# A 31-tap convolution as float32 column-group products on TensorE, and new x made tile by tile behind a normed output

## The chip, the core and the metric

The kernel runs on one core of one Trainium2 chip. The metric is the device time of one launch in microseconds (us), the median of several runs. The core has TensorE for matrix products, VectorE, ScalarE and GpSimd for elementwise work, and SyncE, whose queue here issues the DMA transfers. The profile calls them PE (PEld for its weight loads), DVE, ACT, POOL and SP.

## The reference, cut to what matters

Two transformer blocks run one after the other on x of 512 tokens by 1024 channels. Block 1 has three parts, each followed by a norm of its output and an addition to x; block 2 has six (half-weighted swiglu layers, a pooling mixer and latent attention), added without such a norm.

```python
def first_block(x, mem, ...):
    h = rmsnorm(x, norm_mix_pre)
    y = parallel_mixer(h, ...)
    x = x + rmsnorm(y, norm_mix_post)
    h = rmsnorm(x, norm_mem_pre)
    y = memory_cross_attention(h, rmsnorm(mem, mem_norm_g), ...)
    x = x + rmsnorm(y, norm_mem_post)
    h = rmsnorm(x, norm_ffn_pre)
    y = conv_gated_ffn(h, ...)
    x = x + rmsnorm(y, norm_ffn_post)

def parallel_mixer(h, w_in, conv_dw, conv_dw_b, ...):
    z = h @ w_in
    a = a_val * sigmoid(a_gate)               # 512 channels of z
    a = dwconv_centred(a, conv_dw, conv_dw_b) # depthwise, 31 taps, centred
    a = silu(layernorm(a, ...))
    q, k = rope(rmsnorm(q, ...)), rope(rmsnorm(k, ...))
    att = gqa(q, k, v)                        # 8 heads, 2 kv heads
    return concat([a, att]) @ w_out
```

## The kernel before

Activations lie with channels on the partitions: x is eight tiles of 128 channels by 512 tokens. A product is made from exact parts: a float32 operand is split into a high part `hi` that fp32r keeps, and the rest `lo`, and `mm3` sums three matmuls (hi·hi, hi·lo, lo·hi). Weights come from DRAM in units of 128 x 1024 (`fetch`, on SP's queue, into three buffers `raw`); `cook` makes `hi` on ACT and `lo` on DVE or, for a share of `wshare` fourths of the units, on POOL (`W_IN`, `W_KV`: all of them for the in-projection and for the memory's keys and values). `linear` runs over output tiles, and each of them over the input tiles.

**The mixer** first makes 14 output tiles of the in-projection (`ORDER`): four pairs of gate and value, whose product is the convolution's input `at`, one tile of k, one of v, four of q. Then come eight heads of attention, one head ahead: `scores` (products, maximum on DVE, exponential on ACT), `attend` (transposes and products on PE). Between the heads stand two units of the memory's key and value projection (`mem_kv`, after `mem_prep`), and at the end the product with `w_out`. The convolution has four channel tiles. Of the 31 taps of a tile six are PE products with diagonal matrices (`conv_pe`, tile `dg` from POOL), one is an ACT operation and 24 are DVE operations of the form acc = at * w + acc (`conv_taps`). It is a generator, a tap a step; `step` takes six taps behind every output tile of the in-projection, 30 behind the last, eight behind each head, and `issue_after` pins them behind a named instruction. `conv_norm` follows, at the heads `CN_AT`.

**Behind each of block 1's three parts** stands a settling. `post_collect` evacuates the part's output as y (times the norm's gain) with its squares; `settle`, called from `pre` of the next part, sums the squares on PE, makes the reciprocal root on DVE in 4-column operations, and broadcasts it with four PE products into PSUM (`bc`). ACT copies this to SBUF (`rs`); DVE makes y·rs of tiles 0 and 1 and POOL those of tiles 2 to 7; DVE adds each y to its x tile. `split` then makes `xh` (ACT) and `xl` (DVE), ACT makes the squares and POOL adds them up (`gather`). While PE waits it runs 25 bf16 products that nobody reads (`warm`). The order of work on each engine comes from the scheduler, within these dependences.

The lines of the profile's rows are the 24 taps' line (`acc` from `at`, `cwh`), the diagonals' line (`dg`), the addition in `settle` (`x` from `x`, `y`), the low part in `split_into` (`xl`), and the low part of weights in `cook` (`wlo`).

Of the kernel before, what the change touches and what calls it, by code (L numbers as in the profile page):

```python
# [17 lines left out]
P = 128  # L18
# [8 lines left out]
# order of the taps' offsets: the even ones from the middle, then the odd ones  # L27
TAPS = sorted(range(-(KTAPS // 2), KTAPS // 2 + 1), key=lambda d: (d % 2, abs(d), d))
# [5 lines left out]
_VECS = [  # L34
    ("g_mix", 8), ("conv_w", 4 * KTAPS), ("conv_b", 4), ("cln_g", 4), ("cln_b", 4),
# [25 lines left out]
class Kern:  # L61
# [3 lines left out]
    def __init__(self, ctx, tc, a, out):  # L65
# [10 lines left out]
                      for n, b in (("xs", 16), ("cv", 9), ("pr", 2), ("m", 16), ("q", 17), ("t", 7),  # L76
                                   ("tb", 4))}
# [25 lines left out]
    # -- small access helpers --  # L103
# [10 lines left out]

    def ps(self, tag="ps", name="ps"):
        return self.pps[tag].tile([P, S], F32, name=name, tag=tag)
# [40 lines left out]
    def load_tile(self, w, nt, nk):  # L157
        """Stationary tiles of output tile nt: list over k of (hi, lo) [P, P]."""
# [6 lines left out]
    def mm3(self, ps, w, x, start, stop):  # L165
        """ps += w.T @ x with w, x each given as exact (hi, lo) parts."""
# [14 lines left out]
    # -- split an fp32 tile (SBUF or PSUM), optionally scaled per partition --  # L181
# [31 lines left out]
    def columns(self, sm, dim, eps=0.0, w=1):  # L213
        """sm / dim + eps in columns [P, block, w], in PSUM."""
# [8 lines left out]
    def newton(self, v, n):  # L223
        """rsqrt of v [P, n] on the vector engine."""
# [14 lines left out]
    def rstd(self, sqs, dim, nb=4):  # L239
        """rsqrt(mean + eps) in columns from squares [P, nb * P], summed over the list."""  # L240
        sm = self.sums([(self.c("ones"), sq) for sq in sqs], nb)
# [26 lines left out]
    def bcast_ps(self, R, nb=4, w=1):  # L268
        """Columns to rows of all partitions (row r of w in its share of them), exact float32."""
# [14 lines left out]
    def expand(self, R, w, tag="t"):  # L284
        """Columns -> [32 * block + r, tokens], zero outside the block, as exact parts."""
# [13 lines left out]
    def spread(self, X, r, tag="mi"):  # L299
        """Row r of every block, on all partitions."""  # L300
# [6 lines left out]
    # -- residual stream --  # L307
# [5 lines left out]
    def gather(self, sqs, sq, last, w=S):  # L313
        """Sum of squares so far: at most two tiles, the last one kept apart."""
# [5 lines left out]

    def pre(self, gname, dve_squares=(), tag2="xs"):
# [27 lines left out]
    def settle(self):  # L349
        """Generator: adds the pending normed output to x, a tile a step."""  # L350
# [22 lines left out]
    SETTLE = 2  # L373
# [32 lines left out]
    def rope(self, src, g, gs, cos, sin):  # L406
        """Rotary embedding along the partitions (pairs 16 apart), gains g, gs folded in."""
# [11 lines left out]
    def stack(self, src, r, tag, on_pool=False):  # L419
        """Exact parts of the 64 rows src[64 r:], one in each half of a tile."""  # L420
# [27 lines left out]
    def mem_prep(self):  # L448
        """Gain times memory as exact parts."""
# [14 lines left out]
    def mem_kv(self):  # L464
        """Generator: key and value projections of the memory, a weight unit a step."""
# [927 lines left out]
```

## Time and profile before

| | |
|---|---|
| time, median of 3 runs | 2588.05 us (2588.05 to 2589.86) |
| span of the profiled execution | 2588.3 us |
| PE busy | 2496.1 us, 96% of the span |
| DVE busy | 1385.5 us, 54% |
| ACT busy | 919.1 us, 36% |
| POOL busy | 521.8 us, 20% |
| mixer (start to the last product with `w_out`) | 0 to 321 us |
| first settling | 321 to 354 us |
| memory part | to 460 us |
| second settling | 460 to 497 us |
| conv-gated feed-forward | to 841 us |
| third settling | 841 to 878 us |
| block 2 | to 2588 us |

Matmuls are pipelined: the record of a 512-column matmul is 0.39 us long, while the next one starts about 0.23 us later, so the share of busy time says only where PE stood still, and the granted clock (PEclk, 1.00 is 2.4 GHz, 0.50 is 1.2 GHz) where it ran slowly. A float32 matmul leaves two records, an fp32r one a single record. Idle time is listed with the instruction that ended it.

### The profile page before, as it was taken

How to read it: one execution, taken by the hardware profiler on the slowest of the kernel's cores; microseconds unless marked ns; L12 is line 12 of the kernel's file. 1: busy time of each engine (PE TensorE's matmuls, PEld its weight loads, DVE VectorE, ACT ScalarE, POOL GpSimd, SP SyncE). 2: the span in 40 equal slices, each digit the busy share in tenths (PEclk: the TensorE clock that was granted, in tenths of full speed). 3: DMA queues.
4: the chain of work that ended last, by engine and by line, in shares of the span. 5: the costliest groups of instructions: out<-in, count | busy, mean ns of one | idle time of the engine just before them, and what ended most of it. 6: DMA issues, size and time to landing. Idle time of an engine off the chain costs nothing.

```text
span 2588.3 us, 29365 instructions
## 1 busy us (share of the span) xinstructions
PE 2496.1 (96%) x11668; PEld 2037.2 (79%) x11668; DVE 1385.5 (54%) x1877; ACT 919.1 (36%) x1332; POOL 521.8 (20%) x417
## 2 busy tenths in 40 slices
PE   7879989899999899999999999999999999999999
PEld 6667768688888688888888888888887778888887
DVE  7997563686632645533655543555433576555522
ACT  3336534354422333322422322323222455422221
POOL 4575232311100311101211100111000144111100
PEclk9889999999999999999999999999999999999999
DMA  4211211133333222234232333223332210333232
GB/s 163 66 67 49 90 57 58 64 98 98 96 95 97 69 94 96 95 98 132 74 98 98 97 98 96 97 95 95 98 98 88 78 62 19 104 98 97 92 107 79
DMA packets 68201, 229.80 MB, mean 89 GB/s; under 512 B 7456, under 2 KB 9632, under 8 KB 68064
## 3 DMA queue, kind: packets, MB, share of 16 engines
q1 hardware_dynamic: 66688, 225.35, 27.1%
q0 software_dynamic: 1232, 2.36, 0.3%
q8 instruction: 91, 1.49, 0.2%
q14 instruction: 46, 0.38, 0.0%
q10 hardware_dynamic: 144, 0.23, 0.0%
HBM read 225.80 MB, written 2.10 MB: 88 GB/s over the span
## 4 chain that ended last, share of the span: by engine, by line
PE 86%; DVE 4%; ACT 1%; issue 0%; ACTq 0%
PE ps L169 26%; PE ps L168 26%; PE ps L170 26%; DVE x L369 1%; DVE xl L190 1%; PE wo L168 1%; PE wo L169 1%; PE wo L170 1%; PE pt L124 1%; PE po L169 0%; PE bc L274 0%; PE po L168 0%; PE po L170 0%; PE sc L168 0%; DVE wlo L140 0%
## 5 line engine op out<-in xcount | busy, mean ns | idle before, releaser
L138 ACT CAST whi<-raw 128x1024 fp32r<-128x1024 f32 (+2 forms) x432 | 440.5, 1021 | 1217.7 <-PE ps L169 767.5
L140 DVE TENSOR_TENSOR wlo<-raw,whi 128x1024 fp32r<-128x1024 f32 (+2 forms) x400 | 559.3, 1400 | 492.6 <-ACT whi L138 487.5
L169 PE MATMUL ps<-xl,whi 128*128 128x512 f32 x2008 | 789.8, 394 | 18.6 <-DVE xl L190 18.5
L168 PE MATMUL ps<-xh,whi 128*128 128x512 f32 x2008 | 784.9, 393 | 15.0 <-ACT xh L189 14.7
L170 PE MATMUL ps<-xh,wlo 128*128 128x512 f32 x2008 | 786.6, 392 | 0.0
L169 PEld LDWEIGHTS ps<-xl,whi 128*128 128x128 f32 x2008 | 380.5, 189 | 104.6 <-DVE xl L190 25.0
L168 PEld LDWEIGHTS ps<-xh,whi 128*128 128x128 f32 x2008 | 379.7, 189 | 97.3 <-ACT xh L189 16.2
L170 PEld LDWEIGHTS ps<-xh,wlo 128*128 128x128 f32 x2008 | 380.7, 190 | 79.8 <-issue 0.9
L168 PE MATMUL ps<-ah,whi 128*128 128x512 f32 x880 | 342.3, 389 | 0.0
L169 PE MATMUL ps<-al,whi 128*128 128x512 f32 x880 | 342.3, 389 | 0.0
L170 PE MATMUL ps<-ah,wlo 128*128 128x512 f32 x880 | 342.3, 389 | 0.0
L877 DVE TENSOR_TENSOR g<-ps,bct 128x512 f32<-128x512 f32 x176 | 120.6, 691 | 389.9 <-PE ps L170 382.8
L882 POOL TENSOR_TENSOR g<-g 128x512 f32<-128x512 f32 x88 | 119.0, 1353 | 856.5 <-ACT whi L138 457.6
L317 POOL TENSOR_TENSOR sq<-sq 128x512 f32<-128x512 f32 x72 | 112.7, 1566 | 535.8 <-ACT sq L310 533.9
L170 PEld LDWEIGHTS ps<-ah,wlo 128*128 128x128 f32 x880 | 165.2, 188 | 34.4
L169 PEld LDWEIGHTS ps<-al,whi 128*128 128x128 f32 x880 | 165.2, 188 | 34.2
L168 PEld LDWEIGHTS ps<-ah,whi 128*128 128x128 f32 x880 | 165.2, 188 | 34.2
L556 DVE SCALAR_TENSOR_TENSOR acc<-at,cwh,acc 128x502 f32<-128x502 f32 (+12 forms) x96 | 114.1, 1201 | 1.0 <-ACT acc L548 0.5
L140 POOL TENSOR_TENSOR wlo<-raw,whi 128x1024 fp32r<-128x1024 f32 x32 | 81.3, 2542 | 71.4 <-ACT whi L138 71.2
L185 ACT CAST ah<-g 128x512 fp32r<-128x512 f32 x88 | 54.7, 622 | 112.8 <-POOL g L882 112.8
L387 DVE SCALAR_TENSOR_TENSOR x<-ps,x 128x512 f32<-128x512 f32 x40 | 27.5, 691 | 84.5 <-PE ps L170 84.4
L858 POOL TENSOR_TENSOR c<-c 128x512 f32<-128x512 f32 x22 | 29.7, 1348 | 208.3 <-DVE c L845 178.5
(298 smaller groups left out, 2594.8 us busy)
## 6 DMA issues: line engine op xcount, KB each, us to landing
raw<-in_wgu SPq DMA_DIRECT2D x176, 512.0 KB, 3.5
raw<-in_wd SPq DMA_DIRECT2D x64, 512.0 KB, 3.5
raw<-in_w_up SPq DMA_DIRECT2D x44, 512.0 KB, 3.5
raw<-in_wd SPq DMA_DIRECT2D x32, 384.0 KB, 3.1
raw<-in_w_down SPq DMA_DIRECT2D x16, 512.0 KB, 3.5
raw<-in_w_in SPq DMA_DIRECT2D x14, 512.0 KB, 4.0
raw<-in_mla_w_in SPq DMA_DIRECT2D x9, 512.0 KB, 3.5
raw<-in_mla_w_q SPq DMA_DIRECT2D x12, 384.0 KB, 3.0
```

Of the source, the lines that this page charges most:

```text
L138: self.nc.scalar.copy(hi[:, s], raw[:, s])
L140: eng.tensor_tensor(out=lo[:, s], in0=raw[:, s], in1=hi[:, s].bitcast(F32), op=ALU.subtract)
L168: mm(ps, w[0], x[0], start=start, stop=False)
L169: mm(ps, w[0], x[1], start=False, stop=False)
L170: self.mmi = mm(ps, w[1], x[0], start=False, stop=stop)
L185: nc.scalar.copy(hi, src)
L317: self.nc.gpsimd.tensor_tensor(out=sqs[0][:, :w], in0=sqs[0][:, :w], in1=sq[:, :w], op=ALU.add)
L387: self.nc.vector.scalar_tensor_tensor(out=self.x[nt], in0=ps, scalar=scale, in1=self.x[nt], op0=ALU.mult, op1=ALU.add)
L556: nc.vector.scalar_tensor_tensor(out=acc[:, o], in0=at[:, s], scalar=w(n), in1=acc[:, o], op0=ALU.mult, op1=ALU.add)
L858: nc.gpsimd.tensor_tensor(out=c, in0=c, in1=st["g"], op=ALU.mult)
L877: nc.vector.tensor_tensor(out=g, in0=ps, in1=rb, op=ALU.mult)
L882: nc.gpsimd.tensor_tensor(out=g, in0=g, in1=st["g"], op=ALU.mult)
```

## The change

**The convolution** leaves DVE, ACT and POOL. Each tile of 128 channels is taken as four groups of 32. For group c a tile `cx[c]` holds its 32 channels four times, shifted by 0, 8, 16 and 24 tokens, each copy on 32 partitions: 16 DMAs a channel tile (SBUF to SBUF, on SP's queue). A stationary matrix of 128 x 32 from a new input `conv_d` then applies four taps at a time, and eight steps m, which read `cx[c]` from column m on, make 32 taps. Each product is a float32 matmul, whose 32 output rows are one column group of the array: 4 tiles x 8 steps x 4 groups = 128 matmuls of 512 columns. `conv_d` (4 x 512 KB) comes through `fetch`, and its buffer is held until the tile's last product. ACT evacuates the sum. The four tiles' convolutions stand behind heads 0, 0, 1 and 2 (`CONV_AT`), the norm's three parts behind heads 4, 5 and 6; all `step` and `issue_after` calls of the convolution are gone.

**The low parts of weights** in the in-projection and in the memory's projections are all made on DVE (`W_IN`, `W_KV` = 0).

**The settling** drops the copy `rs` and POOL's products: DVE multiplies each y tile by `bc` in PSUM and adds it to x, and ACT and DVE split the tile at once; `chain` pins this order on DVE and on ACT. The squares of all eight tiles go to PE, eight groups of four matmuls in place of two.

**Tiles.** The pool `tb` (4 x 2048 bytes a partition) becomes `big` (2 x 4608 bytes); the rope tables of block 1 move to `cv`, those of block 2 and a key pair of latent attention share the big tiles; the packed vector loses its 124 columns of taps. All later pools stand 512 bytes lower, so that the remainder of an address by 512 stays and that by 2048 does not.

The diff, cut:

```diff
     def pre(self, gname, dve_squares=(), tag2="xs"):
+        if self.pending is not None:
+            return self.pre_settle(gname, tag2)
         xs, sqs = [], []
-        settle = self.settle()
         for k in range(ND):
-            next(settle, None)
...
+    def pre_settle(self, gname, tag2):
+        nc = self.nc
+        xs, sqs = [], []
+        settle, pin = self.settle(), self.chain()
+        for k in range(ND + 1):
+            if k < ND:
+                for ins in next(settle):
+                    pin(ins)
+                hi, lo = self.t("xs", F32R, name="xh"), self.t(tag2, F32R, name="xl")
+                pin(nc.scalar.activation(hi, self.x[k], AF.Copy, scale=self.v(gname, k)))
+                xs.append((hi, lo))
+            if k:
+                hi, lo = xs[k - 1]
+                x = self.x[k - 1]
+                pin(nc.vector.scalar_tensor_tensor(out=lo, in0=x, scalar=self.v(gname, k - 1),
+                                                   in1=hi.bitcast(F32), op0=ALU.mult,
+                                                   op1=ALU.subtract))
+                sq = self.t(name="sq")
+                pin(nc.scalar.activation(sq, x, AF.Square))
+                sqs.append(sq)
+                if k % 4 == 0:
+                    if k == 4:
+                        ps = self.ps("mi", "sum")
+                    sm = self.sums([(self.c("ones"), q) for q in sqs], ps=ps, start=k == 4,
+                                   stop=k == ND)
+                    sqs = []
+        return xs, self.rsqrt(sm, D)
...
         rb = self.bcast_ps(R)
         self.warm(wps, self.WARM[2])
-        rs = self.t(name="rs")
-        nc.scalar.copy(rs, rb)
-        for k in range(self.SETTLE, ND):
-            nc.gpsimd.tensor_tensor(out=st["y"][k], in0=st["y"][k], in1=rs, op=ALU.mult)
         for k in range(ND):
             y = st["y"][k]
-            if k < self.SETTLE:
-                nc.vector.tensor_tensor(out=y, in0=y, in1=rb if k == 0 else rs, op=ALU.mult)
-            nc.vector.tensor_tensor(out=self.x[k], in0=self.x[k], in1=y, op=ALU.add)
-            yield
+            yield [nc.vector.tensor_tensor(out=y, in0=y, in1=rb, op=ALU.mult),
+                   nc.vector.tensor_tensor(out=self.x[k], in0=self.x[k], in1=y, op=ALU.add)]
...
-    W_IN, W_KV, W_OUT, W_MEM = 4, 4, 0, 1
+    W_IN, W_KV, W_OUT, W_MEM = 0, 0, 0, 1
...
+    def conv_room(self):
+        self.cx = []
+        for _ in range(2):
+            x = self.big("cx").rearrange("p (c u) -> p c u", c=2)[:, :, :S + STEPS]
+            self.nc.gpsimd.memset(x[:, :, :HALO], 0.0)
+            self.nc.gpsimd.memset(x[:, :, S + STEPS - 1 - HALO - 1:], 0.0)
+            self.cx += [x[:, 0], x[:, 1]]
+
+    def conv(self, i, at):
+        nc = self.nc
+        wd = self.fetch(self.a["conv_d"][i], UNIT)
+        W = S + STEPS - 1
+        for c in range(4):
+            for j in range(SHIFTS):
+                o = STEPS * j - HALO
+                u0, u1 = max(0, -o), min(W, S - o)
+                nc.sync.dma_start(out=self.cx[c][32 * j:32 * j + 32, u0:u1],
+                                  in_=at[32 * c:32 * c + 32, u0 + o:u1 + o])
         ps = self.ps(self.CP_TAG, "cps")
...
+        for m in range(STEPS):
+            for c in range(4):
+                o = (4 * m + c) * 32
+                nc.tensor.matmul(ps[32 * c:32 * c + 32, :], wd[:, o:o + 32],
+                                 self.cx[c][:, m:m + S], start=m == 0, stop=m == STEPS - 1)
+        acc = self.t("cv", name="acc")
+        nc.scalar.activation(acc, ps, AF.Identity, scale=0.5, bias=self.v("conv_b", i))
+        return acc
```

Of the old convolution the diff removes the six products and diagonals of `conv_pe` and the taps of `conv_taps`.

On PE, in the in-projection, where the first channel tile's diagonal products (`cps`, from the split input `ahh`, `ahl`) lie between the projection's (`ps`, from `xh`, `xl`), before:

```order
L168 MATMUL ps<-xh,whi 128x512
L168 MATMUL cps<-ahh,dg 128x512
L169 MATMUL ps<-xl,whi 128x512
L170 MATMUL ps<-xh,wlo 128x512
L168 MATMUL ps<-xh,whi 128x512
L169 MATMUL cps<-ahl,dg 128x512
L170 MATMUL cps<-ahh,dg 128x512
L168 MATMUL cps<-ahh,dg 128x510
L169 MATMUL cps<-ahl,dg 128x510
L170 MATMUL cps<-ahh,dg 128x510
L168 MATMUL cps<-ahh,dg 128x510
```

So it goes on for 18 products a tile, split among the projection's. After the change the in-projection has none of them, and the convolution's products stand between heads of attention. Here, on PE behind the first head, is the second tile's (`cps`, from `cx` and the raw weights), among scores (`sc`), transposes (`pt`) and head outputs (`po`):

```order
L696 MATMUL sc<-kh,st 128x512
L697 MATMUL sc<-kl,st 128x512
L587 MATMUL cps<-cx,raw 32x512
L176 MATMUL po<-pth,vh 128x512
L177 MATMUL po<-ptl,vh 128x512
L178 MATMUL po<-pth,vl 128x512
L132 MATMUL pt<-con,p 128x128 x4
L696 MATMUL sc<-kh,st 128x512
L697 MATMUL sc<-kl,st 128x512
L587 MATMUL cps<-cx,raw 32x512
L696 MATMUL sc<-kh,st 128x512
```

The products have moved behind the first heads. Three of the second tile's 32 stand alone between attention's products, and the other 29 follow in one piece some rows further on; the third and the fourth tile have the same 1 + 1 + 1 + 29, and the first tile 15 + 3 + 14.

On DVE, in the first settling, from the first product y·r on (`bc` is the broadcast root, `rs` its copy in SBUF), before:

```order
L368 TENSOR_TENSOR y<-y,bc 128x512
L368 TENSOR_TENSOR y<-y,rs 128x512
L369 TENSOR_TENSOR x_116<-x_116,y 128x512
L369 TENSOR_TENSOR x_118<-x_118,y 128x512
L369 TENSOR_TENSOR x_117<-x_117,y 128x512
L369 TENSOR_TENSOR x_119<-x_119,y 128x512
L190 SCALAR_TENSOR_TENSOR xl<-x_116,vec,xh 128x512
L369 TENSOR_TENSOR x_120<-x_120,y 128x512
L190 SCALAR_TENSOR_TENSOR xl<-x_117,vec,xh 128x512
L190 SCALAR_TENSOR_TENSOR xl<-x_118,vec,xh 128x512
L369 TENSOR_TENSOR x_121<-x_121,y 128x512
```

The additions run ahead of the low parts here. On DVE at the same place after the change:

```order
L418 TENSOR_TENSOR y<-y,bc 128x512
L419 TENSOR_TENSOR x_116<-x_116,y 128x512
L418 TENSOR_TENSOR y<-y,bc 128x512
L419 TENSOR_TENSOR x_117<-x_117,y 128x512
L378 SCALAR_TENSOR_TENSOR xl<-x_116,vec,xh 128x512
L418 TENSOR_TENSOR y<-y,bc 128x512
L419 TENSOR_TENSOR x_118<-x_118,y 128x512
L378 SCALAR_TENSOR_TENSOR xl<-x_117,vec,xh 128x512
L418 TENSOR_TENSOR y<-y,bc 128x512
L419 TENSOR_TENSOR x_119<-x_119,y 128x512
L378 SCALAR_TENSOR_TENSOR xl<-x_118,vec,xh 128x512
```

Before, only two of the products y·r are DVE's; now it does y·r, x + y and the low part of the tile before in turn, 24 operations in a row.

## Rows read from the trace of the kernel before

**Rows 1.** The page, its first part: engine, busy us (share of the span), instructions.

```profile
PE 2496.1 (96%) x11668; PEld 2037.2 (79%) x11668; DVE 1385.5 (54%) x1877; ACT 919.1 (36%) x1332; POOL 521.8 (20%) x417
```

**Rows 2.** The page, its fourth part: chain that ended last, share of the span by engine.

```profile
PE 86%; DVE 4%; ACT 1%; issue 0%; ACTq 0%
```

**Rows 3.** Busy time by stretch: start:end length, engine busy (instructions), PEclk granted, DMA share, GB/s.

```profile
60.00:100.00 40.00, 31.80 (x161) 24.35 (x162) 38.98 (x50) 14.30 (x22) 19.90 (x15) 0.91 0.30 93
100.00:140.00 40.00, 33.47 (x147) 26.36 (x146) 40.00 (x51) 11.86 (x23) 20.88 (x13) 0.87 0.13 46
140.00:200.00 60.00, 39.92 (x232) 35.95 (x231) 58.25 (x82) 20.41 (x33) 48.97 (x28) 0.80 0.21 71
...
260.00:322.00 62.00, 59.40 (x286) 47.20 (x284) 33.53 (x50) 33.73 (x53) 16.29 (x10) 1.00 0.28 94
322.00:351.00 29.00, 17.27 (x80) 10.10 (x80) 25.08 (x29) 11.51 (x20) 21.77 (x13) 0.88 0.05 18
...
460.00:484.00 24.00, 15.91 (x73) 9.15 (x71) 20.00 (x24) 9.36 (x15) 16.43 (x11) 0.79 0.07 24
...
841.00:858.00 17.00, 9.00 (x55) 4.11 (x53) 12.99 (x20) 6.83 (x11) 9.74 (x7) 0.89 0.16 55
```

**Rows 4.** What PE waited for, 0 to 330 us: total us, times, longest.

```profile
PE ps L168 <- DVE mk L479: 9.9, 2, 7.7
...
PE bc L274 <- DVE y L235: 7.0, 2, 6.3
PE bc L274 <- DVE f L261: 5.2, 1, 5.2
```

**Rows 5.** The page, its fifth part: low parts of weights, the taps; busy us, mean ns, idle before.

```profile
L140 DVE TENSOR_TENSOR wlo<-raw,whi 128x1024 fp32r<-128x1024 f32 (+2 forms) x400 | 559.3, 1400 | 492.6 <-ACT whi L138 487.5
...
L556 DVE SCALAR_TENSOR_TENSOR acc<-at,cwh,acc 128x502 f32<-128x502 f32 (+12 forms) x96 | 114.1, 1201 | 1.0 <-ACT acc L548 0.5
```

**Rows 6.** Groups of POOL, 0 to 322 us: form, count, busy us, mean ns, idle before.

```profile
L140 POOL TENSOR_TENSOR wlo<-raw,whi 128x1024 fp32r<-128x1024 f32 x28 | 71.7, 2564 | 46.4 <-ACT whi L138 46.2
...
L530 POOL TENSOR_TENSOR dg<-con,cws 128x512 fp32r<-128x512 f32 x12 | 16.0, 1339 | 6.9 <-PE cps L170 6.8
```

**Rows 7.** Order of time on PE at four places: start us, us, instruction.

```profile
15.12 1.74 PE L208 MATMUL sum<-sq,con 128*32 128x128 f32 x56
...
31.48 1.05 PE L274 MATMUL bc<-con,y 128*128 128x128 f32 x8
...
235.56 1.12 PE L745 MATMUL mean<-tot,con 128*128 128x512 f32 x2 [0.75 <-DVE tot L743]
...
2036.50 1.52 PE L208 MATMUL ksum<-sq,con 128*32 128x128 f32 x48
```

**Rows 8.** DMA issues: operands, queue, count, KB each, median us from issue to landing.

```profile
raw<-in_w_in SPq DMA_DIRECT2D x14, 512.0 KB, 4.0
...
outT<-x SPq DMA_DIRECT2D x8, 256.0 KB, 2.0
```

**Rows 9.** The line `x += y`, all uses: duration ns min/median/max, first and last start.

```profile
L369 DVE TENSOR_TENSOR x<-x,y x24: 679/1752/1780, 330.1 to 867.5; 128x512 f32<-128x512 f32 x24
```

**Rows 10.** Order of time on DVE in the first settling, 328 to 352 us.

```profile
328.32 0.69 DVE L368 TENSOR_TENSOR y<-y,bc 128x512 f32<-128x512 f32 x1 [1.99 <-ACT rs L362]
...
345.89 0.68 DVE L369 TENSOR_TENSOR x<-x,y 128x512 f32<-128x512 f32 x1
346.50 0.74 DVE L190 SCALAR_TENSOR_TENSOR xl<-x,vec,xh 128x512 fp32r<-128x512 f32 x1
347.16 1.78 DVE L369 TENSOR_TENSOR x<-x,y 128x512 f32<-128x512 f32 x1
348.86 3.08 DVE L190 SCALAR_TENSOR_TENSOR xl<-x,vec,xh 128x512 fp32r<-128x512 f32 x3
```

**Rows 11.** Order of time on PE at that settling's end.

```profile
353.98 0.39 PE L169 MATMUL ps<-xl,whi 128*128 128x512 f32 x1
354.21 0.39 PE L170 MATMUL ps<-xh,wlo 128*128 128x512 f32 x1
```

More of the change, by code (lines that the diff above doesn't have):

```diff
@@ L26 @@
 KTAPS = 31
-TAPS = sorted(range(-(KTAPS // 2), KTAPS // 2 + 1), key=lambda d: (d % 2, abs(d), d))
+HALO = KTAPS // 2
+SHIFTS, STEPS = 4, 8
 UNIT = 1024
@@ L113, in t, with big @@
         return self.pools[tag].tile([P, w], dt, name=name, tag=tag)
+    BIG = 9 * P
+    def big(self, name, dt=F32):
+        return self.bigp.tile([P, self.BIG], dt, name=name, tag="big")
     def ps(self, tag="ps", name="ps"):
@@ L239, in rstd, with rsqrt @@
     def rstd(self, sqs, dim, nb=4):
-        sm = self.sums([(self.c("ones"), sq) for sq in sqs], nb)
+        return self.rsqrt(self.sums([(self.c("ones"), sq) for sq in sqs], nb), dim, nb)
+    def rsqrt(self, sm, dim, nb=4):
         v = self.columns(sm, dim, EPS)
@@ L319, in gather, with chain, pin @@
         return sqs
+    def chain(self):
+        last = {}
+        def pin(ins):
+            if ins.ins.engine in last:
+                self.tc.add_manual_dep(
+                    ins.ins, last[ins.ins.engine].name,
+                    mybir.DependencyInfo(mybir.DependencyClass.NoSync,
+                                         mybir.DependencyReason.DATA), reason="chain")
+            last[ins.ins.engine] = ins.ins
+            return ins
+        return pin
     def pre(self, gname, dve_squares=(), tag2="xs"):
+        if self.pending is not None:
+            return self.pre_settle(gname, tag2)
         xs, sqs = [], []
-        settle = self.settle()
         for k in range(ND):
-            next(settle, None)
             xs.append(self.split(self.x[k], self.v(gname, k), "xs", tag2, name="x"))
@@ L542, in conv_taps @@
-    def conv_taps(self, i, at, acc):
-        nc = self.nc
-        w = lambda n: self.cwh[:, i * KTAPS + n:i * KTAPS + n + 1]
-        first = KTAPS // 2
-        o, sl = self.tap(first)
-        nc.scalar.activation(acc[:, o], at[:, sl], AF.Identity, scale=w(first),
-                             bias=self.v("conv_b", i))
-        nc.gpsimd.tensor_copy(acc[:, :1], self.v("conv_b", i))
-        ps = None
-        for m, n in enumerate(n for n in range(self.NPE, KTAPS) if n != first):
-            if m == self.PE_AT:
-                ps = self.conv_pe(i, at)
-            o, s = self.tap(n)
-            nc.vector.scalar_tensor_tensor(out=acc[:, o], in0=at[:, s], scalar=w(n),
-                                           in1=acc[:, o], op0=ALU.mult, op1=ALU.add)
-            yield
-        nc.vector.tensor_tensor(out=acc, in0=ps, in1=acc, op=ALU.add)
+    W_IN, W_KV, W_OUT, W_MEM = 0, 0, 0, 1
@@ L563, in mixer @@
         a = self.a
[L564 removed]
         ws0 = {0: self.tiles(self.cook(self.raw0, UNIT, 4), 8)}
         xs, R1 = self.pre("g_mix", (1, 3, 5))
[L567 to L574 removed]
+        cos, sin = self.t("cv", name="cos1"), self.t("cv", name="sin1")
+        self.conv_room()
         rb = self.bcast(R1)
         st = {}
[L578 removed]
         def ev_gate(nt, ps):
@@ L584, in ev_gate @@
             st["g"] = g
-        convs = []
-        accs = []
-        def step(n):
-            while n and convs:
-                try:
-                    next(convs[0])
-                    n -= 1
-                except StopIteration:
-                    convs.pop(0)
+        ats, accs = [], []
         def ev_val(nt, ps):
-            i = nt // 2
             at = self.t("cv", name="at")
-            acc0 = self.t("cv", name="acc0")
             nc.vector.tensor_tensor(out=at, in0=ps, in1=rb, op=ALU.mult)
@@ L603, in ev_val @@
                                            op1=ALU.mult)
[L604 to L605 removed]
+            ats.append(at)
         ks, vh = [], []
@@ L667, in mixer @@
                 self.mem_prep()
-            step(self.STEP_IN)
         fcol = self.inner_rstd(qsum[:, :P], 64, R1, 8, post=64.0 ** -0.5)
         self.wshare = self.W_KV
-        after = self.last.ins
         self.kv = self.mem_kv()
-        with self.tc.issue_after(after):
-            step(self.STEP_PRE)
         mix = []
@@ L713, in mixer @@
             attend(n)
-            with self.tc.issue_after(self.mxi.ins):
-                step(self.STEP_HEAD if n < self.CN_AT[0] else 1000)
+            for i in range(4):
+                if n == self.CONV_AT[i]:
+                    accs.append(self.conv(i, ats[i]))
             for _ in range(self.KV_HEAD):
                 next(self.kv)
-            for i in range(3):
-                if n == self.CN_AT[i]:
-                    with self.tc.issue_after((self.loi if self.CN_AF[i] else self.mxi).ins):
-                        next(cn)
+            if n in self.CN_AT:
+                next(cn)
         self.wshare = self.W_OUT
@@ L1334, in host_arrays @@
         .reshape(2, 4, P, UNIT))
+    w = f("conv_dw")[0].reshape(KTAPS, 4, 4, 32)
+    cd = np.zeros((4, SHIFTS, 32, STEPS, 4, 32), np.float32)
+    for d in range(KTAPS):
+        for c in range(32):
+            cd[:, d // STEPS, c, d % STEPS, :, c] = w[d, :, :, c]
+    out["conv_d"] = cd.reshape(4, P, UNIT)
     out["rope1"] = _axial_rope()
```

55 lines of the change are left out of this document (9 added, 46 removed).

## The prediction

> **What bounds the kernel now.** I read the shares of the engines first, then the chain that ended last, then PE's idle time by stretch, then what ended it. PE is busy 96% of the span [rows 1] and holds 86% of the chain, DVE 4% [rows 2]. So the kernel is a stream of matmuls, 0.23 us from one to the next [rows 11], and a change pays only where PE stands still, runs at a lower clock, or does work that goes away. Two places show such time [rows 3].
>
> The first is the mixer from 60 to 200 us. PE is busy 31.80 + 33.47 + 39.92 = 105.2 of 140 us, so 34.8 are idle. The granted clock is 0.91, 0.87 and 0.80, between its levels of 2.4 and 1.2 GHz; at full clock the same stretches would lose up to 40 x 0.09 + 40 x 0.13 + 60 x 0.20 = 20.8 us less. Together 55.6. In that time DVE is busy 38.98 + 40.00 + 58.25 = 137.2 of 140: it is the bound. Of PE's idle time 9.9 + 6.3 + 5.2 = 21.4 us end on DVE results that have nothing to do with the convolution (the memory's keys, two root chains) [rows 4]; they queue behind the 96 taps, 114.1 us [rows 5]. From 260 on PE is idle for 2.6 of 62 us, the taps being done.
>
> The second is the settling. The three stretches show 29.0 - 17.3 = 11.7, 8.1 and 8.0 us of idle time and, by the clocks 0.88, 0.79 and 0.89, up to 3.5 + 5.0 + 1.9 more: 38 us in all, which bounds the gain there. DVE's `x += y` takes 679 ns at best and 1752 in the middle of 24 [rows 9], 0.68 beside 1.78 us within 1.3 us of time [rows 10].
>
> **The mixer, term by term.** PE loses 72 diagonal products, 72 x 0.23 = 16.6 us. It gains 128 float32 products of 512 columns on 32-column groups, which the trace has only with 128 columns: 56 records (28 matmuls) take 1.74 us, 48 (24 matmuls) 1.52 [rows 7]; the difference, 0.22, is the price of four, one in each group. For 512 columns that is 4 x 0.22 = 0.88 us a quad, 32 x 0.88 = 28 us. That holds in one piece. A product alone is nearest to the lone full-width float32 matmul, 1.12 us with its ends [rows 7]. Tiles two to four have three such singles and 29 in one piece: 3 x 1.12 + 7.25 x 0.88 + 0.3 for entry = 10.1 each; the first tile, 15 + 3 + 14, 8.5 x 0.88 and three entries, some 9. The sum is 39, and I take 40, with 28 and 48 as ends. PE's work grows by 40 - 16.6 = 23.4 us.
>
> The same rows show four column groups at 1.74 / 28 = 0.062 us a matmul where full-width ones take 1.05 / 4 = 0.26, a factor of four. The Trainium skill, TensorE: Matmul & The Clock Gate, section "Measured speedup vs the span model", gives 2.38 for three column tiles, 0.79 of the ideal; by an estimate from that page the 28 us would be 35.5 and the time 7 us longer. The trace's rows are for this form at a quarter of its length, and I go by them.
>
> DVE loses the 114.1 us and takes over 28 low parts of weights that POOL made at 2.56 us [rows 6]; at DVE's mean of 1.40 [rows 5] that is 39 us, so that from 60 to 200 it has at most 137.2 - 114.1 + 39 = 62 of 140 us to do. POOL loses 71.7 + 16.0 us [rows 6], and with it most of what slowed DVE. So I expect the 55.6 us to go, except for what the order keeps. The chain of the queries' root still stands between projection and attention, since its small operations follow each other: 4 us, and 3 at the lower clock behind it. The second tile's shifts can be issued only when the first tile's products have read `cx`; they go one by one on SP's queue, where a 256 KB transfer from SBUF lands 2.0 us after issue and a 512 KB one into it after 4.0 [rows 8]. PE then stands at the tile's first product, with scores, transposes and head outputs queued behind it; between the two tiles lie six score products, 1.4 us, and four of the 16 shifts suffice for the first group, so I take 2.3 us, ends 0 and 6. Behind the shifts on SP wait two fetches of memory keys; their products come a head later, which covers them. For the third and fourth tile a head of some 15 us covers the shifts, and if that cover is gone they cost the same 2.3 each. Hand-overs between heads: 2. That is 11.3 us back. The mixer gains 55.6 - 23.4 - 11.3 = 20.9 us; ends 0 and 35.
>
> **The settling.** DVE now does three operations a tile: y·r 0.69, the addition 0.68, the low part 0.74, each as it is when POOL is quiet [rows 10]: 2.11 a tile, 16.9 for eight. ACT's part is two operations a tile and stays behind that. The copy to SBUF goes, so DVE starts some 0.6 us earlier, at 327.7, and ends at 344.6; before, its last low part ends at 348.86 + 3.08 = 351.9 [rows 10] and PE's last product starts at 354.21 [rows 11]. With 1.5 us for the last tile's products PE is through at 346, 8.4 us earlier. The 24 additional square sums cost 24 x 0.062 = 1.5 us, mostly inside waits; I count 0.4. Three settlings give 3 x 8.0 = 24 us. The ends: 12, if DVE's operations stay half as slow as now, and 30, the 38 us bound less the root chains that remain.
>
> **What costs nothing.** The moved pools keep their address's remainder by 512; by 2048 it changes. No row prices that. One ns a matmul would be 11.7 us over 11668 records [rows 1], in either direction; I take 0. Latent attention is ordered slightly differently, 0, within 3 either way.
>
> **The sum.** The profiled execution's span is 2588.3, the median of the runs 2588.05: the same. 2588.3 - 20.9 - 24 = 2543.4, and the gain is 44.9. I say 2544.
>
> **Rivals.**
> First, the other side: column groups of 512 columns do not run together. Then 128 products take 128 x 0.88 = 113 us in place of 28, and the time is 2544 + 85 = 2629, slower. The place is the four runs of `cps` behind heads 0 to 2. It decides from (28 + 45) / 128 = 0.57 us a product. Against it speak the 128-column rows, a quarter of the length. 5%.
>
> Second, weight loads are exposed: each product waits for its own stationary matrix, and costs what the lone one has over its stream, 1.12 - 0.88 = 0.24, so 31 us and 2575. The rows show 24 products, each with its load, in 1.52 us [rows 7], too short for that. 4%. The Trainium skill, TensorE: Matmul & The Clock Gate, section "The mechanism", says that weight loads overlap with matmuls in flight only where the row group differs, and column groups share theirs; these rows disagree at 128 columns, and no row shows 512.
>
> Third, attention takes the mixer's gain back: with the taps gone nothing fills the first heads, PE waits on the softmax between scores and transposes and runs at the lower clock, as it did around its waits at 140 to 200 (0.80 [rows 3]). For it: PE is in order, and a late shift stops all. Against it: from 260 on heads run with 2.6 us idle in 62. Then 2544 + 21 = 2565. 18%.
>
> Fourth, the settling gains little, because DVE stays slow for a reason other than POOL, or one operation per step in strict order exposes the hand-over between DVE and ACT: 6 in place of 24, 2562. 9%.
>
> Fifth, better: singles cost no more than in a quad (-12), shifts are hidden (-2), settlings give 27: about 2526. 12%.
>
> Sixth, addresses: 1 to 2 ns a matmul, 2532 or 2567. 4%, half each.
>
> **How the numbers follow.** The forecast keeps 48%, less 1% for what I don't see, which I put on the slower side: with the first rival 6%. No change needs the third and fourth at once: 3%, taken out of theirs. A measurement tells 0.2%, 5 us, from no change, so faster is 91%. For the range the exposed loads (2575), serial groups (2629) and the best few per cent are left out: 2518 to 2572.
>
> **What would show it.** In the profile after: the `cps` group starts some 0.22 us apart a product in its long pieces (0.88: first rival; 0.45: second); DVE under 60% busy from 60 to 200; PE idle for under 15 us there, clock near 1; the mixer's last product at about 300; `x += y` at 0.68 in all 24 uses; the products with the last low parts done about 346 - 321 = 25 us after the mixer's end, and again 28 after the memory part's. The forecast is wrong if PE's idle time moves from DVE's to SP's or ACT's releases, or if matmuls elsewhere start further apart than 0.23 us.

## The result, and the profile after

The changed kernel takes 2557.11 us (2555.78 to 2557.76, four runs) beside 2588.52; the ratio is 0.9878, with a 95% interval from 0.9864 to 0.9891. So it is 31 us faster. The forecast was 2544, the range 2518 to 2572: the direction and the range hold, and the gain is 13.5 us short of the 44.9.

The profiled execution has a span of 2554.0 us and a time of 2555.78, 1.8 more; that of before, with a span of 2588.3, then stands at about 2590, the upper end of its runs. Between the two spans lie 34.3 us. The table has the stages in us, from the starts of PE's records. A settling starts at the first product that nobody reads (`warm`) and ends at the start of the named product of the next part:

| | before | after | difference |
|---|---|---|---|
| mixer | 321.1 | 309.4 | -11.7 |
| first settling, to the 48th product with x | 33.1 | 25.7 | -7.4 |
| memory part | 106.1 | 106.1 | 0 |
| second settling, to the 72nd product with x | 36.7 | 27.8 | -8.9 |
| conv-gated feed-forward | 344.2 | 344.0 | -0.2 |
| third settling, to the 72nd product | 36.8 | 27.8 | -9.0 |
| block 2, to the last product's start | 1705.9 | 1708.8 | +3.0 |

The page's first part (busy us, share of the span, instructions) and its fourth (chain that ended last) answer to [rows 1, 2]:

```profile
PE 2502.4 (98%) x11996; PEld 2019.6 (79%) x11996; DVE 1272.0 (50%) x1819; ACT 916.6 (36%) x1324; POOL 372.0 (15%) x339
...
PE 95%; DVE 3%; ACT 1%; issue 0%; DMA 0%; ACTq 0%
```

DVE has lost 114 us and PE's share of the chain rises from 86 to 95%. The stretches that answer to [rows 3] (start:end length, PE, PEld, DVE, ACT, POOL busy, granted clock, DMA share, GB/s):

```profile
60.00:100.00 40.00, 40.00 (x227) 31.65 (x225) 24.86 (x45) 19.71 (x34) 15.65 (x12) 1.00 0.37 120
100.00:140.00 40.00, 30.00 (x170) 15.86 (x170) 22.18 (x61) 15.50 (x35) 16.07 (x18) 0.91 0.08 20
140.00:200.00 60.00, 60.00 (x400) 34.21 (x401) 27.29 (x56) 26.05 (x48) 10.86 (x14) 1.00 0.45 136
200.00:260.00 60.00, 54.43 (x273) 43.30 (x271) 37.28 (x69) 28.01 (x49) 13.10 (x12) 0.94 0.28 88
260.00:310.00 50.00, 46.34 (x207) 36.23 (x208) 21.56 (x28) 27.89 (x44) 9.27 (x6) 1.00 0.23 74
```

From 60 to 100 us nothing is lost any more, and DVE is no longer full. But PE is idle for 10 us from 100 to 140, at a clock of 0.91, and the stretch from 200 to 260 now has 5.6 us idle and 0.94. Before, that stretch lost little:

```profile
200.00:260.00 60.00, 57.58 (x291) 44.92 (x290) 43.07 (x106) 42.26 (x87) 29.25 (x32) 1.00 0.14 44
```

What PE waited for from 95 to 310 us (total, times, longest), the two largest, answers to [rows 4]:

```profile
PE sc L696 <- ACT p L448: 13.7, 7, 6.7
PE po L177 <- DVE ptl L195: 2.3, 5, 0.7
```

No listed wait ends on a root or on the memory's keys any more. The softmax (ACT's exponential, which frees the scores' PSUM tiles) has come in their place, which is the prediction's own sign of being wrong: idle time that moves to ACT's releases. The longest of these waits is still a root chain. In order of time, on three engines:

```profile
104.85 2.59 POOL L474 TENSOR_TENSOR st<-m,st 64x512 fp32r<-64x512 f32 x2 [0.73 <-ACT st L472]
...
106.19 1.30 DVE L242 TENSOR_TENSOR b<-b,y 128x32 f32<-128x32 f32 x1
107.52 1.26 POOL L195 TENSOR_TENSOR mkl<-mk,mkh 128x512 fp32r<-128x512 f32 x1
107.53 1.30 DVE L243 SCALAR_TENSOR_TENSOR y<-b,y 128x32 f32<-128x32 f32 x1
108.86 0.19 DVE L240 SCALAR_TENSOR_TENSOR b<-y,v 128x32 f32<-128x32 f32 x1
...
110.69 0.78 ACT L448 ACTIVATE p<-sc,nb,f 128x512 f32<-128x512 f32 x1 [4.64 <-DVE nb L446]
...
111.61 0.80 PE L696 MATMUL sc<-kh,st 128*128 128x512 f32 x1 [6.71 <-ACT p L448]
```

PE waits for the exponential, and the exponential for the queries' root on DVE. Three operations of that chain take 0.87, 1.30 and 1.30 us, each until an operation of POOL ends; the later ones take 0.19 each. That is 2.9 us of the wait. Meanwhile SP's queue issues nothing from 94.9 to 131.5 us (the start of each group):

```profile
94.57 0.33 SPq L137 DMA_DIRECT2D raw<-in_conv_d  x1
131.54 10.03 SPq L581 DMA_DIRECT2D cx<-at  x16
141.61 6.79 SPq L137 DMA_DIRECT2D raw<-in_w_mem_k  x2
```

It stands on the second tile's shifts, which wait for the first tile's products. Behind them comes the third unit of key weights, at 141.6. Before, the third to fifth were issued at 116.2, 126.9 and 132.3 us. So by the transition only the first two units of keys have been fetched.

The convolution on PE, in order of time (start us, us, instruction):

```profile
123.06 3.63 PE L587 MATMUL cps<-cx,raw 128*32 128x512 f32 x30
...
136.12 1.05 PE L587 MATMUL cps<-cx,raw 128*32 128x512 f32 x2
137.10 0.66 PE L132 MATMUL pt<-con,p 128*128 128x128 f32 x4
...
144.89 7.06 PE L587 MATMUL cps<-cx,raw 128*32 128x512 f32 x58
```

58 records are 29 products: 7.06 us, 0.24 a product with the ends (the forecast had 0.22 and 0.3 us for entry). A single product occupies PE from 136.12 to 137.10, 0.98 us; 1.12 was taken. The start-to-start times of all 256 records add up to 37.9 us, where 40 was taken.

The settling on DVE, its beginning in order of time, and all uses of `x += y` (duration ns min/median/max), answering to [rows 10, 9]:

```profile
315.94 0.69 DVE L418 TENSOR_TENSOR y<-y,bc 128x512 f32<-128x512 f32 x1 [1.31 <-PE bc L284]
316.66 0.69 DVE L419 TENSOR_TENSOR x<-x,y 128x512 f32<-128x512 f32 x1
317.27 0.68 DVE L418 TENSOR_TENSOR y<-y,bc 128x512 f32<-128x512 f32 x1
317.98 0.69 DVE L419 TENSOR_TENSOR x<-x,y 128x512 f32<-128x512 f32 x1
318.59 0.75 DVE L378 SCALAR_TENSOR_TENSOR xl<-x,vec,xh 128x512 fp32r<-128x512 f32 x1
```

```profile
L419 DVE TENSOR_TENSOR x<-x,y x24: 691/692/694, 316.7 to 833.3; 128x512 f32<-128x512 f32 x24
```

Each operation runs at 0.69 us, the addition in all 24 uses. The three settlings by stretch, answering to [rows 3]:

```profile
309.40:335.40 26.00, 22.62 (x155) 13.41 (x154) 18.20 (x36) 12.59 (x20) 2.35 (x1) 1.00 0.07 21
441.20:469.20 28.00, 26.72 (x187) 18.66 (x187) 20.48 (x40) 14.28 (x21) 0.00 (x0) 1.00 0.06 20
813.00:841.00 28.00, 26.72 (x187) 18.66 (x187) 20.44 (x40) 14.30 (x21) 0.00 (x0) 1.00 0.09 31
```

The clock is 1.00 in all three, where it was 0.90, 0.86 and 0.86 over the same stretches before. The 64 shifts land 2.0 us after issue (a quarter of them in this row of the DMA issues), and none of PE's waits from 95 to 310 us ends on one, though the queue stood on them as shown above:

```profile
cx<-at SPq DMA_DIRECT2D x16, 64.0 KB, 2.0
```

### The profile page after: what moved, and what is told of

Read it like the earlier page. It is cut to its first block, busy times and chain, and to the rows that moved or that the text cites. A ratio compares the mean times of both kernels' runs of the same rounds, so it can differ in the third digit from the quotient of the medians.

```text
span 2554.0 us, 29962 instructions
## 1 busy us (share of the span) xinstructions
PE 2502.4 (98%) x11996; PEld 2019.6 (79%) x11996; DVE 1272.0 (50%) x1819; ACT 916.6 (36%) x1324; POOL 372.0 (15%) x339
## 4 chain that ended last, share of the span: by engine, by line
PE 95%; DVE 3%; ACT 1%; issue 0%; DMA 0%; ACTq 0%
PE ps L177 28%; PE ps L176 28%; PE ps L178 28%; PE cps L587 1%; PE pt L132 1%; PE po L177 1%; PE sum L216 1%; PE po L176 1%; PE po L178 1%; PE wo L176 1%; PE wo L177 1%; PE wo L178 1%; PE bc L284 1%; PE sc L176 0%; DVE wlo L148 0%
## 5 line engine op out<-in xcount | busy, mean ns | idle before, releaser
L148 DVE TENSOR_TENSOR wlo<-raw,whi 128x1024 fp32r<-128x1024 f32 (+2 forms) x428 | 590.7, 1382 | 517.3 <-ACT whi L146 512.1
L178 PEld LDWEIGHTS ps<-ah,wlo 128*128 128x128 f32 x880 | 165.2, 188 | 34.3
L327 POOL TENSOR_TENSOR sq<-sq 128x512 f32<-128x512 f32 x54 | 81.6, 1512 | 546.2 <-ACT sq L320 545.7
L448 ACT ACTIVATE p<-sc,nb,f 128x512 f32<-128x512 f32 (+3 forms) x80 | 53.4, 673 | 43.3 <-DVE nb L446 39.8
L195 DVE TENSOR_TENSOR al<-g,ah 128x512 fp32r<-128x512 f32 x88 | 63.1, 718 | 10.0 <-ACT ah L193 9.6
L450 POOL TENSOR_SCALAR p<-p,rl 128x512 f32<-128x512 f32 (+3 forms) x80 | 49.4, 623 | 123.0 <-DVE rl L449 120.0
```

Of the source, the lines that this page charges most:

```text
L148: eng.tensor_tensor(out=lo[:, s], in0=raw[:, s], in1=hi[:, s].bitcast(F32), op=ALU.subtract)
L178: self.mmi = mm(ps, w[1], x[0], start=False, stop=stop)
L195: self.loi = eng.tensor_tensor(out=lo, in0=src, in1=hi.bitcast(F32), op=ALU.subtract)
L327: self.nc.gpsimd.tensor_tensor(out=sqs[0][:, :w], in0=sqs[0][:, :w], in1=sq[:, :w], op=ALU.add)
L448: nc.scalar.activation(p[:, :w], ps[:, :w], AF.Exp, bias=nb, scale=f, accum_out=l)
L450: nc.gpsimd.tensor_scalar(out=p[:, :w], in0=p[:, :w], scalar1=rl, scalar2=1.0, op0=ALU.mult, op1=ALU.mult)
```

## The experiments

All times are medians beside runs of the kernel before on the same chip (2588.5 to 2589.9).

**Each part alone.** The first has the changed kernel's convolution with the old settling, the second the old convolution with the new settling.

```diff
 e1 (changed kernel)
-        if self.pending is not None:
-            return self.pre_settle(gname, tag2)
+        settle = self.settle()     # with rs, POOL's products, gather
 e2 (kernel before)
+        if self.pending is not None:
+            return self.pre_settle(gname, tag2)
```

> The changed kernel with the old settling (POOL's products, the copy rs, no pinned order). Theory: the two parts add up, the mixer is worth 321.1 - 309.4 = 11.7 us and the latent attention's shared key tile costs 3, so 2588 - 11.7 + 3 = about 2580, with the mixer's last product at 309 and the settlings as long as in the kernel before (33 to 37 us to the last low part's products). Rival: part of the settlings' gain comes from the conv part (POOL free of low parts of weights), then the settlings are 3 us or more shorter each and the time is under 2572.

> The kernel before with the new settling alone. Theory: three settlings are 7.4, 8.9 and 9.0 us shorter, nothing else moves: 2588 - 25 = about 2563. Rival: the gain needs POOL free, then at most 15 us, 2573 or more.

Measured: 2580.32 (ratio 0.9968, 0.9957 to 0.998) and 2563.93 (0.9905, 0.989 to 0.9919). 8.3 + 24.6 = 32.9 us, where both give 31.4: the parts add up. With the convolution alone the settlings are as long as before (33.1, 36.8, 36.8), with low parts of weights gone from POOL and all. The first settling of this kernel by stretch, PE and so on as above:

```profile
310.50:343.60 33.10, 22.13 (x99) 13.76 (x98) 25.99 (x30) 12.68 (x21) 21.73 (x13) 0.85 0.05 16
```

DVE is busy for 26 us of it and the clock is 0.85, where it was 0.90 before.

**The convolution in one piece.** Reversing the column groups makes PE ask first for the group whose shifts land last.

```diff
         for m in range(STEPS):
-            for c in range(4):
+            for c in reversed(range(4)):
```

> The changed kernel with the four column groups taken in the order 3, 2, 1, 0 at each step, so that the group whose shifts land last is asked for first; PE then has tiles two to four as 32 products in one piece each. Theory (single products between others are what the convolution's price is made of: 37.9 us measured where 28 is the price of full quads): about 8 us less than the changed kernel, 2549. Rival (the singles stand where PE would wait anyway, and softmax latency sets the heads): within 2 us of 2557.

Measured: 2545.42 (0.9833, 0.9818 to 0.9848), 11.7 us better than the changed kernel; its convolution takes 30.1 us in place of 37.9, and the mixer 302.0 in place of 309.4. Tiles two and three in order of time:

```profile
145.88 7.85 PE L587 MATMUL cps<-cx,raw 128*32 128x512 f32 x64
...
165.32 7.30 PE L587 MATMUL cps<-cx,raw 128*32 128x512 f32 x64 [0.29 <-PE po L178]
```

The singles were not standing in waits: the convolution is 7.8 us shorter and the mixer 7.4. 3 of the 11.7 us lie elsewhere, in latent attention (below). The rest is spread between executions: between the two profiled ones lie 10.5 us.

**One column group after the other.**

```diff
-        for m in range(STEPS):
-            for c in range(4):
+        for c in range(4):
+            for m in range(STEPS):
```

> The changed kernel with the loops exchanged, so that the eight products of one column group follow each other. Theory (four groups run together, one group alone does not): 128 products at 0.87 us = 111 in place of 38, so about +70 us, 2627. Rival (the 0.22 us a product has nothing to do with four groups in turn): 2557.

Measured: 2603.86 (one run), 46.8 us slower than the changed kernel, with a convolution of 92.4 us. A piece of one group's eight products, with what follows, and a piece of 24:

```profile
148.21 7.06 PE L587 MATMUL cps<-cx,raw 128*32 128x512 f32 x16
155.20 0.66 PE L132 MATMUL pt<-con,p 128*128 128x128 f32 x4
...
156.71 17.42 PE L587 MATMUL cps<-cx,raw 128*32 128x512 f32 x48
```

Within one group a product takes (155.20 - 148.21) / 8 = 0.87 us against 0.22 in turn, the 0.87 that the theory took. In the longer piece the mean is 17.42 / 24 = 0.73, since around a change of group some records start in pairs, under 0.04 us apart. That is why the whole is 92.4 us, 0.72 a product, and not 111. So it is the four groups that make the price, and the first rival's mechanism is real where the groups do not alternate. The Trainium skill, TensorE: Matmul & The Clock Gate, section "Measured speedup vs the span model", gives 2.38 for three column tiles. The runs give 0.87 / 0.22 = 4.0 for four, at 512 columns, above the 0.79 of the ideal that the prediction took from that page.

**Covering the transition to attention.** On top of the reversed groups, the first tile's convolution moves right behind the in-projection (e5), or two more units of memory keys do (e6).

```diff
 e5
+        after = self.mmi.ins
         scores(0)
+        with self.tc.issue_after(after):
+            accs.append(self.conv(0, ats[0]))
...
-                if n == self.CONV_AT[i]:
+                if i and n == self.CONV_AT[i]:
 e6
+        for _ in range(4):
+            next(self.kv)
         scores(0)
```

> The kernel with the column groups in the order 3, 2, 1, 0 (2545.4), and the first tile's convolution moved from behind head 0 to right behind the in-projection's last product, 32 products in one piece. Theory: the wait of 6.7 us between the first and the second pair of head 0's score tiles is the queries' root chain with nothing to cover it; 7 us of convolution cover it: about 2539. Rival: the same convolution covered the softmax of heads 0 and 1, where it then is missing: 2545, with new waits at the scores of head 1.

> The same order of column groups, and four weight units of the memory's keys in place of two ahead of the first scores (convolution where it was, behind heads 0, 0, 1, 2). Theory: as above, the keys' products (24 of 0.12 us a unit, 5.8 us for two units) cover the chain: 2540. Rival: of the three weight buffers the convolution's matrices hold two, so that the third and fourth units come late, and PE waits for weights in place of the root: 2545 or more.

Measured: 2531.88 (0.9778, 0.9762 to 0.9795) and 2550.17 (0.9851, 0.9836 to 0.9866). e5 gains 13.5 us over e3, twice what was expected. Two stretches of e3, then three of e5:

```profile
100.00:140.00 40.00, 28.82 (x169) 16.25 (x167) 22.33 (x61) 15.06 (x33) 15.88 (x18) 0.88 0.06 16
140.00:200.00 60.00, 57.90 (x428) 39.11 (x429) 29.85 (x60) 28.04 (x51) 11.53 (x15) 0.94 0.47 143
...
100.00:140.00 40.00, 36.87 (x265) 20.77 (x264) 24.30 (x63) 19.04 (x39) 16.44 (x18) 1.00 0.28 78
140.00:200.00 60.00, 60.00 (x413) 44.05 (x412) 35.15 (x69) 31.28 (x55) 14.41 (x16) 1.00 0.42 133
200.00:260.00 60.00, 53.76 (x248) 40.17 (x247) 39.11 (x78) 32.99 (x58) 9.23 (x11) 0.94 0.16 53
```

From 100 to 200 PE stands still for 3.1 us in place of 13.3, of which the wait at the transition was 6.5, and the clock is 1.00 throughout, worth up to 40 x 0.12 + 60 x 0.06 = 8.4 us. From 200 to 260 up to 6.4 us are lost again (in e3 56.57 busy, at 1.00). Behind part of the surplus over the expected 6.4 us likely stands SP's queue: e5's second shifts start at 111.8 us and the third unit of key weights at 121.9, in e3 at 132.9 and 143.1, so that key products stand among head 1's. No run separates the two effects. e6 covers the same wait, yet loses 4.8 us against e3. Its waits from 95 us on:

```profile
PE sc L696 <- ACT p L448: 6.0, 5, 2.0
...
PE ps L178 <- DVE wlo L148: 1.4, 2, 0.8
...
PE cps L587 <- DMA cx<-at: 0.8, 2, 0.4
```

The softmax waits fall from 12.8 to 6.0, but new ones on weights and a root (2.3 us) come, and the clock is 0.94 and 0.97 from 140 to 260. That the weight buffers held by the convolution's matrices are the cause, as the rival said, is likely for the waits on `wlo`: SP fetched two of these matrices from 93.8 us on and the next units of keys only from 106.3. Of the rest no run tells.

**The settling's two halves.** e7 takes the pins away, e11 keeps them and gives the products y·r of tiles 2 to 7 back to POOL.

```diff
 e7
-        return pin
+        return lambda ins: ins
 e11
-            yield [nc.vector.tensor_tensor(out=y, in0=y, in1=rb, op=ALU.mult),
+        nc.scalar.copy(rs, rb)
+        for k in range(2, ND):
+            nc.gpsimd.tensor_tensor(out=st["y"][k], in0=st["y"][k], in1=rs, op=ALU.mult)
```

> The changed kernel without the pins, so that the scheduler orders the settling's operations on DVE and ACT; all else as in the changed kernel. Theory: the settling's gain comes from POOL's absence, the pinned order is worth at most 1 us a settling: 2557 to 2560. Rival: without pins the additions run ahead of the low parts as before, and half the gain goes: 2566 or more.

> The changed kernel with the pinned order of additions, low parts and squares, but the products y * r of tiles 2 to 7 on POOL and the copy rs, as before. Theory (the pinned order is most of the settlings' gain, POOL's neighbourhood little): settlings 1 to 3 us longer than in the changed kernel, 2560 to 2566. Rival (what POOL does beside DVE sets DVE's pace, as the prediction had it): the settlings as long as before, 2575 or more.

Measured: 2572.80 (0.9937, 0.9922 to 0.9952) and 2569.38 (0.9929, 0.9912 to 0.9945). Neither did what its theory said: taking the pins away costs 15.7 us, as e7's rival had it (2566 or more), and POOL's neighbourhood 12.3, between e11's theory and rival.

| | y·r on | settlings 1, 2, 3, us | granted clock in them |
|---|---|---|---|
| before | POOL, unpinned | 33.1, 36.7, 36.8 | 0.90, 0.86, 0.86 |
| e7 | DVE, unpinned | 30.6, 36.4, 36.2 | 0.89, 0.86, 0.91 |
| e11 | POOL, pinned | 29.0, 33.5, 33.8 | 0.94, 0.95, 0.95 |
| changed kernel | DVE, pinned | 25.7, 27.8, 27.8 | 1.00, 1.00, 1.00 |

In e7 the scheduler makes all products, then all additions, then all low parts (DVE in order of time; what PE waited for in the first settling; the second settling by stretch):

```profile
317.59 4.87 DVE L418 TENSOR_TENSOR y<-y,bc 128x512 f32<-128x512 f32 x8 [1.31 <-PE bc L284]
322.38 4.90 DVE L419 TENSOR_TENSOR x<-x,y 128x512 f32<-128x512 f32 x8
327.19 5.39 DVE L378 SCALAR_TENSOR_TENSOR xl<-x,vec,xh 128x512 fp32r<-128x512 f32 x8
```

```profile
PE ps L176 <- ACT xh L373: 3.7, 1, 3.7
```

```profile
445.30:482.00 36.70, 31.61 (x189) 20.68 (x189) 22.70 (x51) 13.46 (x22) 0.00 (x0) 0.86 0.11 40
```

DVE is through after 15.0 us (317.59 to 327.19 + 5.39), in the changed kernel after 16.2. But the first addition, which the first high part needs, starts 4.8 us after the first product (322.38) and the first low part 9.6 us after it (327.19), where in the changed kernel it is 0.7 and 2.7 us (315.94 to 316.66 and 318.59). PE stands still for 3.7 us until the first high part is there, and then runs at a lower clock. In e11 the low parts come in turn, but POOL slows DVE in the first half:

```profile
321.28 1.75 DVE L378 SCALAR_TENSOR_TENSOR xl<-x,vec,xh 128x512 fp32r<-128x512 f32 x1
322.96 1.77 DVE L425 TENSOR_TENSOR x<-x,y 128x512 f32<-128x512 f32 x1
...
333.08 1.62 DVE L378 SCALAR_TENSOR_TENSOR xl<-x,vec,xh 128x512 fp32r<-128x512 f32 x2
```

```profile
445.10:478.80 33.70, 30.27 (x189) 19.03 (x189) 22.85 (x36) 14.75 (x23) 9.67 (x6) 0.95 0.10 31
```

Up to 1.77 us an operation until POOL is done, then 0.7; in each settling one wait of 1.6 to 1.9 us, and again a lower clock behind it. Only with both does no wait exceed 0.7 us, and only then is the clock 1.00. One alone gives 3.5 us over the three (e7) or 10.3 (e11), both 25.3. In e7 the memory part behind the first settling is 2.4 us shorter (103.7), so that 5.9 is the fairer number there.

**Low parts of weights on POOL again.** In the changed kernel (e8), in e5's (e9), and in e5's for the memory's keys and values alone (e10).

```diff
-    W_IN, W_KV, W_OUT, W_MEM = 0, 0, 0, 1
+    W_IN, W_KV, W_OUT, W_MEM = 4, 4, 0, 1      # e8, e9; e10: 0, 4, 0, 1
```

> The changed kernel with the low parts of the mixer's weights on POOL again (W_IN and W_KV 4). Theory: DVE is 40 to 60% busy in the mixer after the change and is not its bound, so the side the low parts are made on is worth under 4 us: 2555 to 2561. Rival: POOL's 2.5 us operations stand in the weights' path and slow DVE's beside them, and give back most of the mixer's 11.7 us: 2566 or more.

> The kernel with the first convolution at the transition (2531.9) and the low parts of the mixer's weights on POOL (W_IN and W_KV 4). Theory (an accident of order: what the POOL variant gained over the changed kernel is one softmax wait of 3.5 us with the lower clock behind it, and latent attention's wait, and this kernel has neither at that size): within 3 us of 2531.9. Rival (low parts on DVE stand in front of attention's small operations and cost 6 us as such): about 2525.

> The same with only the memory's keys and values on POOL (W_IN 0, W_KV 4). Accident of order: within 3 us of 2531.9. Rival (DVE's load in attention is what costs, not that in the projection): as the run before, about 2525.

Measured: 2547.13 (0.9839, 0.9824 to 0.9853), 2534.27 (0.9789, 0.9775 to 0.9804) and 2531.88 (0.9781, 0.9766 to 0.9796). e8 is 10 us better than the changed kernel, which neither theory had; 6.6 lie in the mixer, where the softmax wait of 3.3 us at 230 us is absent and the clock from 200 to 260 is 1.00 in place of 0.94 (the wait at the transition is longer, 8.1 us), and 3 in latent attention. In e5's kernel, without that wait at 230, POOL's low parts cost 2.4 us (e9) or nothing (e10). So the side has no price of its own in these runs. That e8's gain is one of order, a wait that falls elsewhere, fits them all but is not shown by itself.

**The convolutions spread.** The 13 us of this expectation are 9.8 by e5's row from 200 to 260: 6.2 idle and 3.6 by the clock.

```diff
-    CONV_AT = (0, 0, 1, 2)
-    CN_AT = (4, 5, 6)
+    CONV_AT = (0, 1, 3, 5)     # on e5
+    CN_AT = (5, 6, 7)
```

> The kernel with the first convolution at the transition (2531.9), the other three behind heads 1, 3 and 5 in place of 0, 1 and 2, and the norm's parts behind heads 5, 6 and 7. Theory: from 200 to 260 us that kernel loses 13 us, in waits of the last heads and at a granted clock of 0.94, because all other work is done by then; spread work gives back 4 to 8: 2524 to 2528. Rival: the convolution's norm comes too late, PE waits for it before the second half of the product with w_out: 2532 or more.

Measured: 2534.79 (0.9787, 0.9771 to 0.9803), 2.9 us slower than e5 and so the rival's number, though not its cause alone. The largest waits of PE:

```profile
PE po L176 <- ACT pth L193: 4.5, 1, 4.5
PE bc L284 <- DVE y L243: 2.3, 1, 2.3
```

One wait for the transposes' evacuation (4.5 us, at 194) takes the place of the former ones; the root of the convolution's norm costs 2.3. The best kernels are e5 and e10, 57 us faster than before.

## Why the prediction was right, and where it was short

**What bounds the kernel: right.** Both places gave, and nothing else moved: matmuls still follow each other at 0.23 us, the memory part, the feed-forward and the swiglu layers are the same within 0.3 us. The addresses' new remainder by 2048 shows no effect.

**The convolution's price: right.** 40 was taken and 37.9 measured, the full pieces at 0.22 a product. Exposed weight loads (the second rival) are excluded by that. The Trainium skill, TensorE: Matmul & The Clock Gate, section "The mechanism", would have loads overlap only where the row group differs; the trace at 512 columns does not agree (29 products, each with a matrix of its own, in 7.06 us). Serial groups (the first rival) did not occur. e4 shows their price, 0.87 a product, though in its order some products still ran together: 50 us in the mixer, not 85.

**What the order keeps in the mixer: the term that was too small.** The sum took 11.3 us: 4 for the root chain and 3 of clock behind it, 2.3 for the shifts, 2 for hand-overs. Measured are 13.7 us of softmax waits (6.7 of them at the root chain) and, by the clocks 0.91 and 0.94, up to 40 x 0.09 + 60 x 0.06 = 7.2 us: 20.9. The difference, 9.6, is about the mixer's shortfall, 9.2 (11.7 in place of 20.9).

Two things stand behind the root chain's 6.7 us. The forecast had POOL lose most of what slowed DVE, but beside POOL three of the chain's operations still cost 2.9 us more than alone; no run takes POOL's work away there. And the forecast let the shifts hold back two fetches of keys at no cost. No wait of PE ends on a shift, but before, 122 of the 192 key products stood between the first and the second scores (138 to 178 us, with waits of 7.7 and 4.3 in them), and now it is 48, the next from 153 us on. It is the third rival's mechanism at half its size. e5 confirms the place: 7.1 us of products there, with the key fetches some 20 us earlier, give 13.5.

With 37.9 and 20.9 in the forecast's own sum the mixer gains 13.4; the 1.7 us to 11.7 stay open. One reading was wrong without harm: DVE was to have at most 62 us to do from 60 to 200, but only 95.9 of the taps' 114.1 us lay there, which makes it 80; it is busy for 74.3.

**The settlings: right in size, half right in cause.** 24 was taken (the forecast's own times give 354.2 - 346.1 = 8.1 where it took 8.4, so 23), 25.3 measured; that the number is so close is in part luck. The forecast explained it by DVE's pace beside POOL alone. e7 has that pace without the pins and gains 3.5; e11 has the pins without it and gains 10.3. What joins them is the clock: over the three settlings the stretches of before lost up to 33 x 0.10 + 37 x 0.14 + 37 x 0.14 = 13.7 us to it, which the forecast used only as a bound, and all of that came back only where no wait was over 0.7 us. The fourth rival, that DVE stays slow, did not occur.

**DVE's additional low parts: right** in e5's kernel, where they cost nothing (e9, e10). In the changed kernel itself POOL's side is 10 us better (e8), which the forecast did not see.

**Latent attention: at the end of its bound.** 3.0 us later, in one wait for a key pair's low part, PE in order of time:

```profile
2081.43 0.58 PE L1138 MATMUL sc<-kp,st 128*128 128x256 f32 x1 [5.48 <-DVE kp L195]
```

Before, that wait was 2.2 us. The kernels with the same tiles wait 2.2 (e3) and 3.5 us (e1) there, and the one with the old tiles 3.5 (e2), so it is not the shared tile that sets it. That the order of DVE and POOL around it does is likely, and not shown.

**The base.** The forecast took the span of before, 2588.3, for the time. With 1.8 us between span and time, that execution took about 2590.1, 1.6 above the median, and the profiled one after the change is 1.3 below its own. So the traces lie 34.3 us apart and the medians 31.4.

The sum by the traces: 11.7 + 25.3 - 3.0 = 34.0 against the 44.9 of the forecast.

## What to carry to other kernels

When work leaves an engine, list the products that stood in the gaps of the engine that bounds, and see where the new order puts them: a wait that was covered comes back, and here a lower clock came with it. Look behind a transfer that must wait, too: what is queued after it waits as well. Make a producer chain deliver its first result early, in the order that the consumer takes them, and pin that order; in e7 the chain's total time was the shorter one. Order column-group products so that the group that is ready last is asked for first, and keep them in one piece.

## What the runs showed of the hardware

- Float32 products of 128 x 32 by 512 columns take 0.22 us each when four column groups alternate, and 0.87 within one group (e4); a lone one among full-width products occupies PE for 0.98.
- The settlings ran at a granted clock of 1.00 where no wait of PE was over 0.7 us, at 0.94 to 0.95 with a longest wait of 1.6 to 1.9 (e11), and at 0.86 to 0.91 with one of 3.7 (e7). The length of a wait alone does not tell: behind the same wait of 2.0 us in the mixer the clock from 133 to 143 us was 1.00 in the changed kernel and 0.83 in e7 and e11.
- The same addition took 0.68 us alone and up to 1.77 beside POOL's product, on one engine within some microseconds (e11). Operations of the root chain on 128 x 32 elements took 0.19 alone and 1.30 beside POOL.
